# Modulation matmuls in column groups, a new load order, and scale and shift of a token tile in one VectorE pass

## The chip, the cores and the metric

The kernel runs on one core of a Trainium2 chip. The metric is the device time of one execution in microseconds; lower is better. The core has five engines with instruction rows of their own: PE (TensorE, matmuls and transposes), DVE (VectorE), ACT (ScalarE), POOL (GpSimd) and SP (SyncE, which here issues the DMAs). Each engine takes its instructions strictly in the order of its row, and one that waits for a semaphore holds up all behind it.

## The reference

One layer of a generator, batch 1, 1024 latent tokens (x) and 256 context tokens (ctx) of width 1024, all in fp32. The change touches only its beginning:

```python
mod_x = (silu_c @ w_ada[layer] + b_ada[layer])[:, None, :]
mod_c = silu_cc @ w_ada[layer] + b_ada[layer]
sh_m, sc_m, gt_m, sh_f, sc_f, gt_f = jnp.split(mod_x, 6, axis=-1)
csh_m, csc_m, cgt_m, csh_f, csc_f, cgt_f = jnp.split(mod_c, 6, axis=-1)
px = modulate(rms_norm(x, g_pre_mix[layer]), sh_m, sc_m) @ w_in[layer]
pc = modulate(rms_norm(ctx, g_pre_mix[layer]), csh_m, csc_m) @ w_in[layer]
```

`modulate(h, shift, scale)` is `h * (1 + scale) + shift`. Behind it come windowed attention, a bidirectional mLSTM, the output projection and a SwiGLU block, whose code is the same in both kernels.

## The kernel before, in words

**Precision.** A large product is made of three fast fp32r matmuls. Each operand is split into a high part (a cast on ScalarE) and a low part (raw minus high, a subtraction on VectorE); `mm3` (L74 to L79) adds high·high, high·low and low·high. In a trace the three carry the lines L77, L78 and L79.

**The modulation vectors** (L304 to L371). For section 1 (scale) and then section 0 (shift) of w_ada, eight row tiles `wa` of 128x1024 (512 KB) are loaded. silu(c) and silu(c_ctx) stand as columns in `cs4` (split) and `cz4` (plain fp32, two more columns zero). In each section three tiles (`PLAIN`, L304) are multiplied in plain fp32; the other five are split by ScalarE and VectorE (L65, L66), with the space of `hh` and `hl` as a scratch. The result `pr` (4 rows of 512, two tiles) is copied into `Vc` and transposed by PE to columns, `pcol`; VectorE adds the bias and leaves `scol` (scale) and `hcol` (shift), one value for each of the 1024 features.

**The token tiles.** There are ten tiles of 128 tokens, eight latent (0 to 7) and two context (8, 9). `prep_a` (L188) loads tile i, sums its squares on ScalarE, takes root and reciprocal, and for the tiles below XT = 6 multiplies by it on GpSimd (tile 2 on ScalarE). `prep_t` (L209) transposes it on PE: eight 128x128 transposes into two PSUM tiles `pt` of half a token tile each, of which there are two at a time (`tp`). `prep_m` (L227) multiplies by the scale on VectorE, one 128x512 pass per half; for tiles from 6 on a transposed copy is loaded and another form is used (L235). `prep_b` (L247) adds the shift (VectorE for tiles 0 and 1, GpSimd behind them), casts to `hh` on ScalarE and subtracts to `hl` on VectorE. `hh` and `hl` have two halves, of four feature blocks each.

**The slabs.** `s1(i)` (L404) multiplies token tile i by `w1` (272 columns: gates, attention V, the first mLSTM head's V): `slab`, eight blocks of three matmuls of 128x272. VectorE adds the gate biases (the two `G` passes), ScalarE copies `av` and `V` out. For slab 0 the order is another: all sixteen matmuls with hh (L391), then the eight with hl (L394). `s2(i)` (L419) multiplies by `w2` (384 columns, the other three heads' V) the first NFILL = 3 tiles; it is interleaved with s1 from i = 3. `w1` is split in `w1_split` (L291), in four casts and four subtractions of 128x544, `w2` at i = 1 and 2 (L452), in four casts and four subtractions of 128x768.

**What sets the order.** Engines' rows are laid down by a scheduler with estimates of its own; instructions in `tc.keep_in_program_order` stay in the order of the program on their engine; `tc.issue_after` holds a DMA back until the named instruction. SP issues the loads in this order: the scale section's eight tiles, two of the shift section, x0, x1, the other six, w1 (two loads), bcr, x2, x3, cst, x4, x5, and the w2 loads between the later tiles. Tiles 0 and 1 are transposed ahead of slab 0, among the shift section's matmuls.

Of the kernel before, what the change touches and what calls it, by code (L numbers as in the profile page):

```python
# [44 lines left out]
def body(tc, x, ctx, xtr, vecs, bcv, bada, gqm, gqf, wada, ws1, ws2, wt, wout, wfi, wfo,  # L45
# [132 lines left out]
    xts, hraw, xd = {}, {}, {}  # L178
# [6 lines left out]
    def prep_a2(i):  # L185
        tc.keep_in_program_order(act.activation(xts[i], xts[i], AF.Copy, scale=st[:, 10 + i:11 + i]))

    def prep_a(i, parts=(0, 1)):  # L188

        j = i - NT  # L190
        xt = xts[i] = R(4 + i % 4, f"xt{i}", (D,))
        xd[i] = dma(xt, x[i * P:(i + 1) * P] if i < NT else ctx[j * P:(j + 1) * P])
        hraw[i] = R((2, 3)[i] if i < 2 else (12, 13, 8, 9, 10, 11)[i % 6], f"hraw{i}", (KT, P))
        if i >= XT:
            dma(hraw[i], xtr[i - XT])
        sq = act.activation(xt if i >= XT else hraw[i].rearrange("p a b -> p (a b)"), xt, AF.Square, accum_out=st[:, i:i + 1])
        if i > 1:
            tc.keep_in_program_order(sq)
        if 1 not in parts:
            tc.keep_in_program_order(act.activation(st[:, 10 + i:11 + i], st[:, i:i + 1], AF.Sqrt, bias=epst, scale=1.0 / D))  # L200
            return
        rms_r(st[:, 10 + i:11 + i], st[:, i:i + 1])
        if i < XT:
            pool.tensor_scalar(xt, xt, st[:, 10 + i:11 + i], 1.0, MUL, MUL)
# [22 lines left out]
    def prep_m(i):  # L227

        if i not in pts:
            prep_t(i)  # L230
        rw = hraw.pop(i)
        raw2[i] = [rw[:, 4 * b:4 * b + 4] for b in range(2)]
        if i >= XT:
            for k in range(KT):
                dve.scalar_tensor_tensor(rw[:, k], rw[:, k], scol[:, i // NT, k:k + 1], pts[i], MUL, MUL)  # L235
            return
        for b in range(2):
            if i == 1 and not b:
                for k in range(4):
                    tc.keep_in_program_order(act.activation(raw2[i][b][:, k], pts[i][b][:, k], AF.Copy,  # L240
                                                                    scale=scol[:, 0, 4 * b + k:4 * b + k + 1]))
                continue
            r = dve.tensor_tensor(raw2[i][b], pts[i][b], hcast(scol[:, i // NT, 4 * b:4 * b + 4]), MUL)
            if i == 1:
                tc.keep_in_program_order(r)

    def prep_b(i):  # L247
# [7 lines left out]
        for b in (1, 0) if i == 0 else range(2):  # L255
            r = (dve if i < 2 else pool).tensor_tensor(raws_[b], raws_[b], hcast(hcol[:, q, 4 * b:4 * b + 4]), ADD)
            if i < 2:
                tc.keep_in_program_order(r)
            if i == 0:
                w1_split(1, (1 - b,))  # L260
        for b in range(2):
            h_ = hs[b][:, :, tok]
            if i + b == 0:
                for k in range(4):
                    act.activation(h_[:, k], pts[i][b][:, k], AF.Identity, scale=scol[:, q, k:k + 1],
                                   bias=hcol[:, q, k:k + 1])
            else:
                tc.keep_in_program_order(act.copy(h_, raws_[b]))
            r = dve.tensor_tensor(ls[b][:, :, tok], raws_[b], h_.bitcast(F32), SUB)
            if i == 0:  # L270
                tc.keep_in_program_order(r)
        if i == 0:
            with tc.issue_after(last):
                prep_a(2, (0,))
            r2 = st[:, 12:13]
            tc.keep_in_program_order(dve.reciprocal(r2, r2))
            prep_a2(2)
# [13 lines left out]
    def w1_split(i, part=None):  # L291

        if part is None or -1 in part:
            for k in (0, 2):
                r = act.copy(w1h[i][:, k:k + 2], w1r[i][:, k:k + 2])
                if part:
                    tc.keep_in_program_order(r)
        for k in (0, 1) if part is None else part if part[0] >= 0 else ():
            sl = slice(2 * k, 2 * k + 2)
            r = dve.tensor_tensor(w1l[i][:, sl], w1r[i][:, sl], w1h[i][:, sl].bitcast(F32), SUB)  # L300
            if part:
                tc.keep_in_program_order(r)

    PLAIN = {1: (0, 2, 4), 0: (0, 2, 7)}  # L304
    last, nsp, late = None, 0, []

    wm = pa.tile([P, 4, P], F32, name="warm", tag="mm", bufs=4)
    for i in range(11):
        pe.matmul(wm[:, i % 4], ones, ones, start=True, stop=True)
    for sec in (1, 0):  # L310
        pr = [pa.tile([4, 512], F32, name=f"pr{sec}{i}", tag="mm", bufs=4) for i in range(2)]
        for kt in range(KT):
# [10 lines left out]
            ops = [(kt, *o) for o in ops]  # L323
            if (sec, kt) > (0, 2) and not sec:
                late += ops
                ops = ()
            if (sec, kt) == (0, KT - 1):

                ops = late = [late[k] for k in (0, 2, 1, 4, 3, 6, 5, 8, 7)]
            for n, (k, a, b) in enumerate(ops):  # L330
                if late and n < 2:
                    prep_t(1, True, (n,))
                for i in range(2):
                    r = pe.matmul(pr[i], a[:, k, :], b[:, i * 512:(i + 1) * 512], start=kt == 0 and n == 0,
                                  stop=kt == KT - 1 and n == len(ops) - 1)
                    if late:
                        tc.keep_in_program_order(r)
            if (sec, kt) == (0, 1):
                for i in range(2):
                    with tc.issue_after(last):  # L340
                        prep_a(i)
                        last = xd[i].ins
            if (sec, kt) == (0, 2):
                prep_t(0, True)
            if (sec, kt) == (0, 7):
                prep_m(0)
                prep_m(1)
                for i in range(2):
                    with tc.issue_after(last):
                        last = w1_load(i)  # L350
                w1_split(0)
                with tc.issue_after(last):
                    last = dma(bcr, bcast(bcv)).ins
        r4 = Vc.rearrange("p n h v -> p (n h v)")[0:4, 0:D]
        r = act.copy(r4[:, 0:512], pr[0])
        if sec == 0:
            tc.keep_in_program_order(r)
            w1_split(1, (-1,))
        dve.tensor_copy(r4[:, 512:D], pr[1])
        pc_ = pa.tile([P, KT, 4], F32, name="pcol", tag="gx", bufs=2)  # L360
        for kt in range(KT):
            pe.transpose(pc_[:, kt, :], r4[:, kt * P:(kt + 1) * P], ident[0:4, 0:4])
        for q in range(2):
            t = (hcol, scol)[sec][:, q]
            if sec:
                dve.scalar_tensor_tensor(t, pc_[:, :, q], 1.0, bcol(1), ADD, ADD)
                dve.tensor_tensor(t, pc_[:, :, 2 + q], t, ADD)
                dve.tensor_tensor(t, t, vec[:, VGPM:VGPM + 8], MUL)
            else:
                for b in (bcol(0), t):  # L370
                    tc.keep_in_program_order(dve.tensor_tensor(t, pc_[:, :, q if b is not t else 2 + q], b, ADD))  # L371
# [32 lines left out]
    def s1(i):  # L404
        ps = slab(i, 272, w1h, w1l)
# [11 lines left out]
    w2h, w2l, s2ps = [], [], {}  # L417
# [11 lines left out]
    prep_b(0)  # L429
    prep_b(1)  # L430
    with tc.issue_after(xd[2].ins):
        prep_a(3, (0,))
    with tc.issue_after(xd[3].ins):
        dma(cst, const)
    for i in range(NI):
        if i + 4 < NI:
            prep_a(i + 4)
        if i == 0:
            s1(i)
            prep_t(2, True)  # L440
        if i + 2 < NI:
            prep_b(i + 2)
        if i == 0:
            r = st[:, 13:14]
            dve.reciprocal(r, r)
            tc.keep_in_program_order(pool.tensor_scalar(xts[3], xts[3], r, 1.0, MUL, MUL))
        if i:
# [1593 lines left out]
```

## Time and profile before

| what | value |
|---|---|
| median of 3 runs | 1171.96 us (1171.68 to 1172.77) |
| the profiled execution | 1171.69 us, span 1169.9 us from first to last instruction |
| mean granted TensorE clock | 0.998 of full speed |
| PE busy | 1155.5 us, 99% of the span |
| DVE, ACT, POOL busy | 782.8, 558.6, 154.5 us |
| slab 0 on PE | 33.94 to 39.27 us |
| slab 1 on PE | 40.14 to 43.23 us |
| HBM traffic over the span | 184 GB/s on average; some 410 GB/s from 5 to 39 us |

Times in the profile are microseconds from the span's start. A row of the timeline gives start, length, engine, line, operation, what it writes and reads, shape, and in brackets how long the engine stood idle before it and what ended that. Matmuls are pipelined: a record's length is a latency, and the distance between starts is the price.

### The profile page before, as it was taken

What the parts mean: (1) busy time and instruction counts of PE and PEld (TensorE: products, weight loads), DVE (VectorE), ACT (ScalarE), POOL (GpSimd) and SP (SyncE); (2) the same over time, 40 slices, a digit from 0 to 9 for tenths busy, and PEclk for the clock granted to TensorE, in tenths of its full rate; (3) what the DMA queues carried; (4) which work ended last, traced back from release to release, by engine and by line L of the source; (5) the groups of instructions that cost most, each with busy time, mean ns of one, the idle gap of its engine ahead of it and who ended that gap; (6) DMA issues with size and microseconds to landing.
All of it is one profiled execution on the core that took longest, in us unless ns stands there. A gap on an engine that the chain in (4) does not pass through costs nothing.

```text
span 1169.9 us, 16222 instructions
## 1 busy us (share of the span) xinstructions
PE 1155.5 (99%) x5857; PEld 945.5 (81%) x5857; DVE 782.8 (67%) x1391; ACT 558.6 (48%) x1037; POOL 154.5 (13%) x201
## 2 busy tenths in 40 slices
PE   9899999999999999999999999999999999999997
PEld 3799888878888767888788888888888888888886
DVE  5874768873787643479777777767677755644557
ACT  6753442223777855877543333334343344434533
POOL 1430001263664630000000000000000000000000
PEclk9999999999999999999999999999999999999999
DMA  9722954657797605220334556566645467665853
GB/s 367 281 68 80 391 175 144 210 170 230 206 254 202 174 10 198 90 83 26 99 135 171 199 206 241 212 201 219 222 143 161 150 212 273 201 208 191 307 181 126
DMA packets 103272, 216.99 MB, mean 185 GB/s; under 512 B 10260, under 2 KB 39572, under 8 KB 101784
## 3 DMA queue, kind: packets, MB, share of 16 engines
q1 hardware_dynamic: 103192, 215.95, 55.5%
q8 instruction: 46, 0.75, 0.3%
q14 instruction: 34, 0.28, 0.1%
HBM read 159.29 MB, written 55.97 MB: 184 GB/s over the span
## 4 chain that ended last, share of the span: by engine, by line
PE 95%; DMA 2%; DVE 2%; issue 0%; ACT 0%; SPq 0%; DVEq 0%
PE xv L79 8%; PE xv L77 8%; PE xv L78 8%; PE pt L78 6%; PE pt L79 6%; PE pt L77 6%; PE t L609 4%; PE t L611 4%; PE t L608 4%; PE pt L1063 3%; PE pt L1045 3%; PE op L77 3%; PE op L78 3%; PE op L79 2%; PE fx L77 2%; PE fx L79 2%
## 5 line engine op out<-in xcount | busy, mean ns | idle before, releaser
L66 DVE TENSOR_TENSOR fo<-fr,fo 128x1024 fp32r<-128x1024 f32 x77 | 92.8, 1223 | 71.4 <-ACT fo L65 69.9
L65 ACT CAST fo<-fr 128x1024 fp32r<-128x1024 f32 x77 | 79.5, 1049 | 74.1 <-PE pt L79 38.2
L608 PE MATMUL t<-hh,th 128*128 128x512 f32 x208 | 82.4, 396 | 0.0
L609 PE MATMUL t<-hl,th 128*128 128x512 f32 x208 | 82.0, 394 | 0.0
L1445 ACT CAST wS<-wr 128x512 fp32r<-128x512 f32 x88 | 54.2, 622 | 55.4 <-PE pt L79 36.8
L1447 DVE TENSOR_TENSOR wS<-wr,wS 128x512 fp32r<-128x512 f32 x88 | 60.4, 689 | 19.7 <-ACT wS L1445 19.7
L79 PE MATMUL xv<-tT,wS 128*128 128x512 f32 x168 | 65.6, 391 | 0.0
L77 PE MATMUL xv<-tT,wS 128*128 128x512 f32 x168 | 65.6, 391 | 0.0
L78 PE MATMUL xv<-tT,wS 128*128 128x512 f32 x168 | 65.5, 390 | 0.0
L611 PE MATMUL t<-hh,tl 128*128 128x512 f32 x208 | 65.0, 393 | 0.0
L77 PE MATMUL op<-woh,mh 128*128 128x512 f32 x128 | 50.9, 397 | 0.0
L79 PE MATMUL op<-woh,ml 128*128 128x512 f32 x128 | 50.0, 390 | 0.0
L78 PE MATMUL op<-wol,mh 128*128 128x512 f32 x128 | 50.0, 390 | 0.0
L1193 DVE TENSOR_TENSOR wr<-wr 128x512 f32<-128x512 f32 x66 | 45.5, 690 | 1.4
L608 PEld LDWEIGHTS t<-hh,th 128*128 128x128 f32 x208 | 39.1, 188 | 8.3 <-issue 0.3
L1479 ACT ACTIVATE es<-es 128x512 f32<-128x512 f32 x22 | 13.9, 633 | 66.6 <-DVE es L1196 66.5
L609 PEld LDWEIGHTS t<-hl,th 128*128 128x128 f32 x208 | 39.1, 188 | 8.0 <-issue 1.2
L77 PE MATMUL pt<-fo 128*128 128x512 f32 x110 | 42.8, 389 | 0.0
L78 PE MATMUL pt<-fo 128*128 128x512 f32 x110 | 42.8, 389 | 0.0
L79 PE MATMUL pt<-fo 128*128 128x512 f32 x110 | 42.8, 389 | 0.0
L611 PEld LDWEIGHTS t<-hh,tl 128*128 128x128 f32 x208 | 37.2, 188 | 6.5 <-issue 0.3
L782 PE MATMUL s<-k,qh 128*128 128x256 f32 (+1 forms) x128 | 41.6, 336 | 0.5 <-DVE sm L784 0.5
(788 smaller groups left out, 3339.3 us busy)
## 6 DMA issues: line engine op xcount, KB each, us to landing
wr<-in_wfi SPq DMA_DIRECT2D x44, 512.0 KB, 5.2
wb<-in_wada SPq DMA_DIRECT2D x24, 512.0 KB, 5.8
s_d<-a SPq DMA_DIRECT2D x22, 512.0 KB, 6.7
bt<-in_wfo SPq DMA_DIRECT2D x44, 256.0 KB, 3.4
tb_d<-bt SPq DMA_DIRECT2D x11, 1024.0 KB, 3.9
fr<-s_d SPq DMA_DIRECT2D x44, 256.0 KB, 4.4
fr<-tb_d SPq DMA_DIRECT2D x44, 256.0 KB, 4.6
fr<-a_d SPq DMA_DIRECT2D x33, 256.0 KB, 4.3
```

Source lines behind the costliest of these rows:

```text
L65: act.copy(hi, raw)
L66: dve.tensor_tensor(lo, raw, hi.bitcast(F32), SUB)
L77: pe.matmul(ps, a[0], b[0], start=first, stop=False, **kw)
L78: pe.matmul(ps, a[0], b[1], start=False, stop=False, **kw)
L79: pe.matmul(ps, a[1], b[0], start=False, stop=last, **kw)
L608: pe.matmul(o, wh[:, kt], m[0], start=f, stop=False)
L609: pe.matmul(o, wh[:, kt], m[1], start=False, stop=False)
L611: pe.matmul(o, wl[:, kt], m[0], start=False, stop=l)
L782: pe.matmul(o, qh[:, h, :], k2[g][:, kc], start=True, stop=False)
L1193: dve.tensor_tensor(out, a, b, SUB)
L1445: act.copy(w[:, 0], raw)
L1447: dve.tensor_tensor(w[:, 1], raw, w[:, 0].bitcast(F32), SUB)
```

## The change

**Modulation.** All sixteen w_ada tiles are multiplied in plain fp32, with `cz`, 32 columns of which two are used. A tile's two halves go to two groups of 32 PSUM rows and columns of the array, and odd row tiles to the other two groups: `pr[g:g+32]`, g = 32·(2·(kt mod 2) + i). One PSUM tile `pr` of 128x512 takes it all; it is copied in two 128x256 pieces and transposed in four 128x128 pieces, and VectorE adds even and odd groups. Small matmuls without use (`warm`, 32 rows, 128 columns) stand between the tiles and around the transposes. The ten casts and ten subtractions of w_ada tiles, the `PLAIN` table and `cs4` are gone.

**Loads.** Only x0 stands among the w_ada tiles. Behind them come w1, x1, x2, bcr, x3, x4, x5, cst, all four w2 pieces (each with a raw tile of its own), then the tiles from 6 on.

**Scale and shift.** For tiles 1 to 5, VectorE reads the transposed tile from PSUM and applies scale and shift in one `tensor_scalar` with two column operands, eight passes of 128x128 for a tile; the two 128x512 multiplications, and the GpSimd additions of tiles 2 to 5, are gone. Tile 0 has code of its own (`prep_b0`).

**Order.** Tile 1 is transposed behind slab 0; tile 2 inside slab 1, tile 4 inside slab 2 (`mid`), with tiles 3 and 5 behind these in the program. The w2 casts and subtractions move from i = 1, 2 to i = 2, 3. `ch`, `cl` are allocated at i = 4.

The core of the diff:

```diff
+    cz = q1.tile([P, KT, 32], F32, name="cz")
...
-            if kt in PLAIN[sec]:
-                ops = ((cz4, w),)
-            else:
-                wh, wl = (t[1 - nsp // 4 % 2][:, nsp % 4] for t in (hh, hl))
-                nsp += 1
-                split(wh, wl, w)
-                ops = ((cs4, wh), (cs4, wl))
...
+            for i in range(2):
+                g = 32 * (2 * (kt % 2) + i)
+                tc.keep_in_program_order(pe.matmul(pr[g:g + 32], cz[:, kt, :], w[:, i * 512:(i + 1) * 512],
+                                                   start=kt < 2, stop=kt > 5))
+            if kt < KT - 1:
+                warm(1)
             if (sec, kt) == (0, 1):
-                for i in range(2):
-                    with tc.issue_after(last):
-                        prep_a(i)
-                        last = xd[i].ins
+                with tc.issue_after(last):
+                    last = prep_l(0)
+                prep_c(0)
...
+            for f in (lambda: w1_load(0), lambda: w1_load(1), lambda: prep_l(1), lambda: prep_l(2),
+                      lambda: dma(bcr, bcast(bcv)).ins, lambda: prep_l(3)):
                 with tc.issue_after(last):
-                    last = dma(bcr, bcast(bcv)).ins
+                    last = f()
...
         for b in range(2):
+            if i:
+                for k in range(4):
+                    kk = 4 * b + k
+                    t = dve.tensor_scalar(rw[:, kk], pts[i][b][:, k], scol[:, 0, kk:kk + 1], hcol[:, 0, kk:kk + 1], MUL, ADD)
+                    tc.keep_in_program_order(t)
+                if i < 4 and b == (i > 1):
+                    prep_c((2, 4, 5)[i - 1], 1)
+            else:
+                dve.tensor_tensor(raw2[i][b], pts[i][b], hcast(scol[:, 0, 4 * b:4 * b + 4]), MUL)
...
     for i in range(NI):
...
         if i == 0:
+            s1(0)
+            prep_t(1, True)
+            prep_c(2, 0)
+            prep_b(1)
...
+        elif i < 3:
+            s1(i, lambda: prep_t(2 * i, True))
+            prep_b(2 * i)
...
+            prep_t(2 * i + 1, True)
+            prep_b(2 * i + 1)
...
-        if i in (1, 2):
-            b = i - 1
+        if i in (2, 3):
+            b = i - 2
```

VectorE's row of before around slab 1, from the end of slab 0 (tile 1 is `hraw_234`, tile 2 `hraw_350`; L243 is the multiplication by the scale, L269 hl, L408 and L410 the G passes):

```order
L408 TENSOR_TENSOR G<-slab,bcr 128x2x4
L410 TENSOR_TENSOR G<-slab,bcr 128x2x4
L269 TENSOR_TENSOR hl_103<-hraw_234,hh_101 128x4x128
L243 TENSOR_TENSOR hraw_350<-pt,scol 128x512
L269 TENSOR_TENSOR hl_104<-hraw_234,hh_102 128x4x128
L243 TENSOR_TENSOR hraw_350<-pt,scol 128x512
L445 RECIPROCAL st<-st 128x1
L408 TENSOR_TENSOR G<-slab,bcr 128x2x4
```

The same place now (tile 1 is `hraw_254`, tile 2 `hraw_257`; L250 is the new pass, L297 hl, L413 and L415 the G passes):

```order
L413 TENSOR_TENSOR G<-slab,bcr 128x2x4
L415 TENSOR_TENSOR G<-slab,bcr 128x2x4
L250 TENSOR_SCALAR hraw_254<-pt,scol,hcol 128x128 x4
L202 RECIPROCAL st<-st 128x1
L250 TENSOR_SCALAR hraw_254<-pt,scol,hcol 128x128 x4
L297 TENSOR_TENSOR hl_103<-hraw_254,hh_101 128x4x128
L297 TENSOR_TENSOR hl_104<-hraw_254,hh_102 128x4x128
L202 RECIPROCAL st<-st 128x1
L413 TENSOR_TENSOR G<-slab,bcr 128x2x4
L415 TENSOR_TENSOR G<-slab,bcr 128x2x4
L250 TENSOR_SCALAR hraw_257<-pt,scol,hcol 128x128 x8
```

In before tile 2 is multiplied between the hl passes of tile 1, ahead of slab 1's G; now the passes of tile 1 stand behind slab 0's G and those of tile 2 behind slab 1's.

ScalarE's row of before at the w2 casts (L460; L268 is a cast to hh, L196 a sum of squares, L412 and L413 the copies from a slab):

```order
L412 COPY av<-slab 128x128
L413 COPY V<-slab 128x128
L460 CAST w2h_477<-wr_0_479 128x768
L460 CAST w2h_477<-wr_2_483 128x768
L196 ACTIVATE xt_487,st<-xt_487 128x1024
L182 ACTIVATE st<-st,epst 128x1 x2
L268 CAST hh_101<-hraw_363 128x4x128
L412 COPY av<-slab 128x128
L413 COPY V<-slab 128x128
L268 CAST hh_102<-hraw_363 128x4x128
L460 CAST w2h_541<-wr_0_543 128x768
L268 CAST hh_101<-hraw_369 128x4x128
```

And now (L473 is the w2 cast, L296 the cast to hh, `hraw_361` is tile 4, `hraw_419` tile 5):

```order
L296 CAST hh_101<-hraw_361 128x4x128
L296 CAST hh_102<-hraw_361 128x4x128
L417 COPY av<-slab 128x128
L418 COPY V<-slab 128x128
L296 CAST hh_101<-hraw_419 128x4x128
L296 CAST hh_102<-hraw_419 128x4x128
L473 CAST w2h_528<-wr_00_421 128x768
L473 CAST w2h_528<-wr_02_423 128x768
L473 CAST w2h_563<-wr_10_425 128x768
L473 CAST w2h_563<-wr_12_427 128x768
```

The first w2 casts stood ahead of the casts of tile 3 (`hraw_363` of before); now all four stand together behind those of tile 5. On PE, the first matmul that reads w2h stands now behind the last transposes of tile 5 (`xt_417`), ahead of slab 4:

```order
L77 MATMUL slab<-w1h_118,hh_102 128x272
L78 MATMUL slab<-w1l_120,hh_102 128x272
L79 MATMUL slab<-w1h_118,hl_104 128x272
L229 MATMUL pt<-vec,xt_417 128x128 x4
L77 MATMUL slab<-w2h_528,hh_101 128x384
L77 MATMUL slab<-w1h_117,hh_101 128x272
L78 MATMUL slab<-w1l_119,hh_101 128x272
```

One matmul of s2 now stands at the head of slab 4; the next that reads w2h follows some twenty rows later.

More of the change, by code (lines that the diff above doesn't have):

```diff
@@ L194, in prep_a, with prep_c @@
         if i >= XT:
[L195 to L204, printed above, removed]
+            with tc.issue_after(w2d[min(i - XT, 1)]):
+                dma(hraw[i], xtr[i - XT])
+        return xd[i].ins
+    def prep_c(i, part=None):
+        xt, r = xts[i], st[:, 10 + i:11 + i]
+        if part in (None, 0):
+            pin = tc.keep_in_program_order if i else lambda r: r
+            pin(act.activation(xt if i >= XT else hraw[i].rearrange("p a b -> p (a b)"), xt, AF.Square,
+                               accum_out=st[:, i:i + 1]))
+            pin(act.activation(r, st[:, i:i + 1], AF.Sqrt, bias=epst, scale=1.0 / D))
+        if part in (None, 1):
+            rc = dve.reciprocal(r, r)
+            if part:
+                tc.keep_in_program_order(rc)
+            if i == 1:
+                tc.keep_in_program_order(act.activation(xt, xt, AF.Copy, scale=r))
+            elif i < XT:
+                pool.tensor_scalar(xt, xt, r, 1.0, MUL, MUL)
+    def prep_a(i):
+        prep_l(i)
+        prep_c(i)
     pts = {}
@@ L289, in w1_load, with w1_split, warm @@
         return dma(w1r[i], ws1[:, i]).ins
[L291 to L307, printed above, removed]
+    def w1_split(i):
+        for k in (0, 2):
+            tc.keep_in_program_order(act.copy(w1h[i][:, k:k + 2], w1r[i][:, k:k + 2]))
+        for k in (0, 2):
+            tc.keep_in_program_order(dve.tensor_tensor(w1l[i][:, k:k + 2], w1r[i][:, k:k + 2],
+                                                       w1h[i][:, k:k + 2].bitcast(F32), SUB))
+    last = None
+    pcols = {1: pa.tile([P, 4, P], F32, name="pcol", tag="gx", bufs=2)}
+    wm = pa.tile([P, 4, P], F32, name="warm", tag="gx", bufs=2)
     for i in range(11):
         pe.matmul(wm[:, i % 4], ones, ones, start=True, stop=True)
+    def warm(n):
+        for i in range(n):
+            tc.keep_in_program_order(pe.matmul(wm[0:32, i % 4], cz[:, 0, :], ones, start=True, stop=True))
     for sec in (1, 0):
-        pr = [pa.tile([4, 512], F32, name=f"pr{sec}{i}", tag="mm", bufs=4) for i in range(2)]
+        pr = pa.tile([P, 512], F32, name=f"pr{sec}", tag="mm", bufs=4)
         for kt in range(KT):
@@ L354, in body @@
-        r4 = Vc.rearrange("p n h v -> p (n h v)")[0:4, 0:D]
-        r = act.copy(r4[:, 0:512], pr[0])
-        if sec == 0:
[L357 to L362, printed above, removed]
+        rr = Vc.rearrange("p n h v -> p (n h v)")[:, 512 * sec:512 * sec + 512]
@@ L363, in body @@
+        for k in range(4):
+            tc.keep_in_program_order(pe.transpose(pcols[sec][:, k, :], rr[:, k * P:(k + 1) * P], ident))
+        if sec == 0:
+            warm(3)
+        pcv = pcols[sec].rearrange("p k (g c) -> p g k c", c=32)
         for q in range(2):
-            t = (hcol, scol)[sec][:, q]
+            if not sec and q:
+                prep_b0()
+            t = (hcol, scol)[sec][:, q].rearrange("p (i k) -> p i k", k=4)
+            b_ = bcol(sec).rearrange("p (i k) -> p i k", k=4)
@@ L402, in vrow, with s1 @@
         return V[:, i] if i < NT else Vc[:, i - NT]
-    def s1(i):
-        ps = slab(i, 272, w1h, w1l)
+    def s1(i, mid=None):
+        ps = slab(i, 272, w1h, w1l, mid)
         sf = i + 2 if i < NT else i - NT
@@ L416, in body @@
     NFILL = 3
-    w2h, w2l, s2ps = [], [], {}
+    w2h, w2l, s2ps, w2r = [], [], {}, {}
     def s2(i, bs=(0, 1)):
@@ L427, in s2 @@
             act.copy(vrow(i)[:, 1:4, 0:128], s2ps.pop(i)[:, 0:384].rearrange("p (h v) -> p h v", v=128))
[L429 to L434, printed above, removed]
+    wc = None
     for i in range(NI):
-        if i + 4 < NI:
-            prep_a(i + 4)
         if i == 0:
[L439 to L447, printed above, removed]
+            s1(0)
+            prep_t(1, True)
+            prep_c(2, 0)
+            prep_b(1)
+            prep_c(3)
+            with tc.issue_after(last):
+                prep_l(4)
+            prep_c(4, 0)
+        elif i < 3:
+            s1(i, lambda: prep_t(2 * i, True))
+            prep_b(2 * i)
+            if i == 1:
+                prep_l(5)
+                with tc.issue_after(xd[5].ins):
+                    last = dma(cst, const).ins
+                for b in range(2):
+                    for k in (0, 2):
+                        raw = w2r[b, k] = R((14 if not b else 0) + k // 2, f"wr384_{b}{k}", (2, 384))
+                        with tc.issue_after(last):
+                            last = w2d[b] = dma(raw, ws2[:, b, k:k + 2]).ins
+                prep_c(5, 0)
+            prep_t(2 * i + 1, True)
+            prep_b(2 * i + 1)
+        else:
+            if 3 < i < NI - 2:
+                prep_b(i + 2)
             s1(i)
```

121 lines of the change are left out of this document (51 added, 70 removed).

## The prediction

> **What bounds the kernel now.** I read the page first, then busy time by windows, then the chain that ended last through the opening, and single instructions for prices. On the page:
>
> ```profile
> span 1169.9 us, 16222 instructions
> PE 1155.5 (99%) x5857; PEld 945.5 (81%) x5857; DVE 782.8 (67%) x1391; ACT 558.6 (48%) x1037; POOL 154.5 (13%) x201
> ```
>
> PE (TensorE) idles only 14.4 us of the span. The change drops no matmul of the slabs, so it can win only PE idle time, PE work that something else could have done, and throttled clock. All three lie in the opening, by windows:
>
> ```profile
> 5.00:30.00 25.00, 23.24 (x90) 6.78 (x89) 16.37 (x22) 14.86 (x22) 2.24 (x2) 1.00 1.02 406
> 30.00:34.00 4.00, 2.22 (x13) 0.79 (x11) 2.89 (x9) 3.33 (x7) 0.11 (x1) 1.00 1.04 408
> ...
> 65.00:70.00 5.00, 5.00 (x37) 5.00 (x36) 5.00 (x19) 2.73 (x8) 3.29 (x5) 1.00 0.01 3
> ```
>
> The columns are busy PE, weight load, VectorE, ScalarE, GpSimd, then granted clock, DMA share and GB/s. From 5 to 34 us DMA is saturated at 406 to 408 GB/s, so 512 KB take 1.29 us; from 65 us PE has no gap that this change could close. The chain in order of time (start, length, what) passes through two loads and then PE:
>
> ```profile
> 9.34 8.96 DMA xt<-in_x
> 18.32 11.56 DMA wr<-in_ws
> ...
> 33.43 0.47 ACT hh L265
> 33.94 3.73 PE slab L391 x16
> 37.68 1.59 PE slab L394 x8
> 39.27 0.87 PE pt L220 x8
> 40.14 0.13 PE slab L77
> ...
> 43.09 0.14 PE slab L79
> 43.25 0.17 DVE G L408
> ```
>
> x0 and x1 stand among the w_ada tiles, w1_0 lands at 29.88, slab 0 runs from 33.94 to 39.27, slab 1 (24 matmuls, 0.129 each) from 40.14 to 43.23. What PE waits for from 33 to 70 us (engine, line, releaser: sum, times, longest):
>
> ```profile
> PE slab L79 <- DVE hl L269: 1.6, 2, 1.5
> ...
> PE slab L391 <- ACT hh L265: 1.0, 1, 1.0
> ...
> PE slab L77 <- ACT hh L268: 0.2, 1, 0.2
> ```
>
> The 1.0 lies ahead of slab 0. Behind it PE waits only 1.8 us: the tile stream is already nearly full.
>
> **The load phase.** The modulation matmuls of before, on PE's timeline, and the only column groups that this trace holds:
>
> ```profile
> 5.46 1.88 PE L334 MATMUL pr<-wa,cz 128*4 128x512 f32 x4
> ...
> 30.72 0.63 PE L334 MATMUL pr<-hl,cs 128*4 128x512 f32 x2
> ```
> ```profile
> 308.40 0.64 PE L1063 MATMUL pt<-ts__3048,av 128*64 128x512 f32 x1
> 308.40 0.64 PE L1063 MATMUL pt<-ts__2895,av 128*64 128x512 f32 x1
> 308.88 0.59 PE L1063 MATMUL pt<-ts__3048,av 128*64 128x512 f32 x1
> ```
>
> A tile in plain fp32 costs 1.88 us on PE today, as four records (each fp32 matmul is two passes). Two matmuls on different 64-column groups start in the same nanosecond, two passes each per 0.9 us. If groups of 32 columns do that too, a w_ada tile costs about 0.9, and a warm matmul, a quarter of the columns of one that costs 0.94, some 0.2: less than the 1.29 in which it arrives. The ten casts and ten subtractions then vanish from the load phase, and with them the backlog that let the last modulation matmul start only at 30.72. The load order takes x1's 512 KB from ahead of w1: w1_0 lands at 29.88 − 1.29 = 28.6, its neighbour w1_1 (544 KB) about 30.0, x1 about 31.3.
>
> ScalarE and VectorE prices for what follows:
>
> ```profile
> 29.90 1.19 ACT L295 CAST w1h<-wr 128x544 fp32r<-128x544 f32 x2 [1.76 <-DMA wr<-in_ws]
> 33.43 1.50 ACT L265 ACTIVATE hh<-pt,hcol,scol 128x128 fp32r<-128x128 f32 x4 [0.61 <-DVE hcol L371]
> 34.81 0.63 ACT L268 CAST hh<-hraw 128x512 fp32r<-128x512 f32 x1
> 35.32 1.08 ACT L196 ACTIVATE hraw<-xt 128x1024 f32<-128x1024 f32 x1
> 36.28 0.21 ACT L196 ACTIVATION_READ_ACCUMULATOR hraw<-xt 128x1 f32 x1
> 36.52 0.29 ACT L200 ACTIVATE st<-st,epst 128x1 f32<-128x1 f32 x1
> 37.46 1.15 ACT L186 ACTIVATE xt<-xt,st 128x1024 f32<-128x1024 f32 x1 [0.64 <-DVE st L276]
> ...
> 52.54 0.83 ACT L460 CAST w2h<-wr 128x768 fp32r<-128x768 f32 x1 [0.94 <-DMA wr<-in_ws]
> ```
> ```profile
> 36.06 1.29 DVE L269 TENSOR_TENSOR hl<-hraw,hh 128x512 fp32r<-128x512 f32 x2
> 37.26 0.16 DVE L276 RECIPROCAL st<-st 128x1 f32<-128x1 f32 x1
> ...
> 61.36 1.62 DVE L235 SCALAR_TENSOR_TENSOR hraw<-hraw,scol,pt 128x128 f32<-128x128 f32 x6
> ...
> 65.14 0.21 DVE L451 TENSOR_SCALAR mF<-cst 128x128 f32<-128x128 f32 x1
> 65.27 0.22 DVE L451 TENSOR_SCALAR mB<-cst 128x128 f32<-128x128 f32 x1
> ```
>
> Slab 0: w1_0 28.6, its two casts to 29.8, first hh quarter 0.47, so PE starts at 30.3. ScalarE is done with hh0 at 31.3, with w1_1's casts at 32.5, with hh1 at 33.1. VectorE then has four passes of 0.65 and a reciprocal (half of w1l1, a shift addition, hl of both halves), ready at 35.3; four matmuls later slab 0 ends at **35.9, 3.4 us ahead of 39.27**.
>
> **The tile stream.** The new pass is an instruction that the kernel already has on another stage, from PSUM with two column operands:
>
> ```profile
> 541.15 1.36 DVE L1274 TENSOR_SCALAR mix<-pt,sfc,hfc 128x128 f32<-128x128 f32 x4
> 542.43 0.68 DVE L1196 TENSOR_TENSOR es<-es,po 128x512 f32<-128x512 f32 x1
> ```
>
> Four take 542.43 − 541.15 = 1.28, 0.32 each, 2.56 for the eight of a tile (TS below). A tile on VectorE is then 2.56 + 1.29 (hl) + 0.25 (two G at the pitch of such small ones) + 0.16 = 4.26 us; on PE it is 3.1 + 0.87 = 3.97. So VectorE, which used to leave half of the modulation to GpSimd, becomes the slower of the two. GpSimd's additions no longer matter to anyone.
>
> [...]
>
> Now tile by tile, in the order that the program sets (rows in the section on the change). I take handoffs as nothing.
>
> - Tile 1 isn't transposed before slab 0 any more. Its square follows hh1 on ScalarE: 33.1 + 1.2 + 0.29, reciprocal, + 1.15 = 35.9; transposes 35.9 to 36.8 (half by 36.4). First four TS to 37.7, cast 0.63: slab 1 starts at 38.4, **wait 1.6**. After two matmuls it needs hl: TS to 39.0, + 0.65 = 39.65, **wait 1.0**. With x2's transposes inside, slab 1 ends at 43.35, where before it ended at 43.23. The head start is gone.
> - Tile 2: VectorE has G of slab 1 ahead of TS, and G waits for slab 1's end; behind it wait all of TS and PE. G to 43.6, four TS to 44.95: x3's transposes need the PSUM buffer, **wait 1.6**. Then cast **0.2**, second half **0.4**, hl **0.35**. Slab 2 ends at 49.9.
> - Tiles 3 and 4: VectorE, never idle now, gives hl(3) at 51.1 and 53.6: **waits 0.05 and 0.5**. Slab 3 ends at 54.9, x5's last transposes at 55.35.
> - The next matmul in PE's row reads w2h. Its cast stands on ScalarE behind both casts of tile 5, these behind TS(5), this behind hl(4) and G of slab 3. From 53.6: three TS, hl, G, hl to 56.1; eight TS to 58.7; cast 59.35; w2h 0.83 to 60.2. **Wait 4.85**, with all of slab 4 queued behind. Before, those casts stand among the tile casts and are early.
>
> Sum: −3.4 for slab 0's end, +0.87 for x1's transposes, which now lie behind it, +10.55 of waits, −1.8 that before waits: **+6.2 us**. The loads behind tile 1 (x2 to x5, cst, w2: some 4 MB, 10 us at that rate) end well before 55 us and cost nothing.
>
> Bounds: VectorE is in an unbroken row from 43.4 to 58.7 with 32 TS, and 8 more matter in tile 1. At the 0.27 of L235 the sum loses up to 2.0; at 0.36 it grows by 1.6. Below 0.29 a tile costs VectorE less than PE, so further savings are lost in part.
>
> **The rivals.**
>
> *The clock drops as well.* In the windows of before:
>
> ```profile
> 35.00:36.00 1.00, 1.00 (x6) 0.79 (x5) 1.00 (x2) 1.00 (x2) 0.00 (x0) 0.72 1.04 414
> 36.00:37.00 1.00, 1.00 (x6) 1.00 (x5) 1.00 (x3) 0.79 (x3) 0.00 (x0) 0.50 1.01 406
> ...
> 38.00:39.00 1.00, 1.00 (x7) 1.00 (x7) 0.61 (x2) 1.00 (x2) 0.00 (x0) 0.57 1.03 399
> ```
>
> After PE's thin stretch at 31 to 34 the clock is halved for some 3.4 us, which costs about 1.7. The new wait of 4.85 is longer and emptier. One drop there gives 7.9, 1179.6 + 0.3; another in slab 1 gives up to 1.7 more. [...]
>
> *Nothing to measure.* If TS costs what L451 shows from SBUF (65.27 − 65.14 = 0.13), PE bounds the stream; tile 1 still waits some 1.0, G and TS of tile 2 another 1.0, w2h 0.25 + 0.65 + 1.04 + 0.63 + 0.83 − 0.44 = 3.0. That makes −3.4 + 0.87 + 5.0 − 1.8 = +0.7, 1172.7. Against it: L451 reads no PSUM and no column.
>
> *Faster.* PE bounds the stream and its waits stay at the 1.8 of before: −3.4 + 0.87 = −2.5, 1169.4. This decides if TS stays below 0.29 and ScalarE reaches w2h before PE does; the order speaks against the second at any price of TS.
>
> *The groups don't run side by side*, so the change doesn't do what it says. Then a tile costs 1.88 + 0.2, above 1.29: 16 of them from 5.46, with x0's transposes and the columns, end near 41 and not 27, and slab 0 starts some 13 later. Tile 1 is then ready (−4): about 1187. Against it: L1063.
>
> **How the numbers follow.** The sum is made on the profiled run, 1171.7, which is 0.3 under the median: 1171.7 + 6.2 + 0.3 = 1178.2. Chances: the sum without a further drop 0.38, with drops 0.34, nothing to measure 0.14, faster 0.07, groups in turn 0.05, the rest (later order) 0.02. A measurement can tell about 0.2%, 2.3 us. Slower: 0.38 + 0.34 + 0.05, with the slow end of the neutral case, 0.78; same 0.14; faster 0.08. The range goes from 1172.5, the neutral case's near end, to 1182.0, two drops.
>
> **What would show it.** Right: slab 0 ending near 36, slab 1 within 1 us of 43.2, TS at 0.32, one PE wait of 4 to 5 us released by a w2h cast, nothing changed behind 90 us. Wrong: a stream without PE gaps, TS near 0.13, w2h cast ahead of its matmul, or modulation matmuls in turn.

## The result and the profile after

Four runs of each kernel: the changed kernel takes 1189.24 us (1186.59 to 1189.77), the kernel before 1172.37 us (1171.68 to 1174.69). The ratio is 1.0136, interval [1.0115, 1.0157]: slower, as forecast, but by 16.9 us and not by 6, and outside the range. The profiled executions that are compared below took 1189.63 and 1171.69 us, a difference of 17.94 us.

The changed kernel's page, span and engines:

```profile
span 1187.8 us, 16250 instructions
PE 1159.6 (98%) x5887; PEld 951.9 (80%) x5887; DVE 769.8 (65%) x1409; ACT 549.9 (46%) x1024; POOL 141.3 (12%) x193
```

PE's idle time grew from 14.4 to 28.2 us, and its busy time by 4.1 us. The first is waits; the second is, for the most part, matmuls that run at half clock, as the windows of the changed kernel show (columns as in the prediction):

```profile
30.00:34.00 4.00, 2.74 (x18) 2.13 (x16) 3.77 (x7) 3.86 (x8) 0.00 (x0) 1.00 0.79 303
34.00:40.00 6.00, 3.43 (x23) 2.58 (x21) 4.79 (x18) 4.02 (x10) 1.12 (x1) 0.99 0.21 72
40.00:45.00 5.00, 4.33 (x19) 4.33 (x20) 1.47 (x4) 3.30 (x7) 1.12 (x1) 0.50 0.97 341
45.00:50.00 5.00, 3.30 (x19) 2.82 (x17) 2.63 (x10) 1.05 (x3) 0.00 (x0) 0.83 0.88 357
50.00:55.00 5.00, 4.89 (x28) 4.79 (x28) 4.97 (x14) 2.66 (x6) 1.42 (x1) 0.66 0.42 132
...
60.00:65.00 5.00, 0.66 (x2) 0.67 (x3) 4.87 (x12) 2.96 (x7) 0.00 (x0) 0.88 0.54 184
65.00:70.00 5.00, 5.00 (x31) 5.00 (x30) 3.04 (x5) 3.88 (x7) 0.00 (x0) 0.78 0.33 105
...
270.00:280.00 10.00, 8.10 (x41) 6.19 (x40) 6.47 (x13) 3.73 (x5) 8.42 (x15) 0.83 0.74 226
```

Read the number behind the five pairs, the granted clock: the rows with 0.50, 0.66 and 0.78 stand behind rows in which PE worked 3.43 of 6.00, 3.30 of 5.00 and 0.66 of 5.00 us. The trace's record of the clock has it halved from 39.9 us for 6.8 us, from 50.1, from 63.8 and from 275.4 for 3.4 us each; before had one such stretch, at 35.4 (and both kernels have one that begins in the last 1.3 us). From 60 to 65 us PE works 0.66 us.

The waits of PE from 28 to 120 us, changed kernel:

```profile
PE slab L77 <- ACT w2h L473: 4.4, 1, 4.4
PE slab L77 <- ACT hh L296: 1.8, 1, 1.8
PE pt L229 <- DVE hraw L250: 1.7, 1, 1.7
PE slab L394 <- ACT hh L277: 1.1, 1, 1.1
PE slab L79 <- DVE hl L297: 1.0, 1, 1.0
```

Every large one is a wait that the prediction had, at its place; the 1.1 lies inside slab 0, where the prediction had it as the time at which the second half of hh is ready. Their starts on PE's timeline, with slab 0's first matmul, its last eight and x1's transposes:

```profile
30.65 0.39 PE L394 MATMUL slab<-w1h,hh 128*128 128x272 f32 x1 [0.18 <-ACT hh L273]
...
34.96 1.42 PE L397 MATMUL slab<-w1h,hl 128*128 128x272 f32 x8 [0.40 <-DVE hl L268]
36.22 1.09 PE L229 MATMUL pt<-vec,xt 128*128 128x128 f32 x8
39.12 0.39 PE L77 MATMUL slab<-w1h,hh 128*128 128x272 f32 x1 [1.81 <-ACT hh L296]
...
40.67 0.59 PE L79 MATMUL slab<-w1h,hl 128*128 128x272 f32 x1 [1.03 <-DVE hl L297]
...
41.29 0.43 PE L78 MATMUL slab<-w1l,hh 128*128 128x272 f32 x1
...
47.05 0.29 PE L79 MATMUL slab<-w1h,hl 128*128 128x272 f32 x1
49.03 0.63 PE L229 MATMUL pt<-vec,xt 128*128 128x128 f32 x4 [1.70 <-DVE hraw L250]
```

Slab 0 ends at 36.2, 3.1 us ahead of before; slab 1 ends at 47.2, 4 us behind before, with two waits ahead of and in it and with matmuls that start 0.23 us apart from 39.9 to 46.7 and 0.13 apart behind that (records of 0.43 and 0.29).

**Where the 17.9 us came from.** I follow the lag of the changed kernel at two marks in PE's row: the first `t<-hh,th`, with which the projections behind the slabs begin, and the first `s<-k,qh`, with which the scores begin. Before, then after:

```profile
118.26 0.39 PE L608 MATMUL t<-hh,th 128*128 128x512 f32 x1
...
283.70 0.38 PE L782 MATMUL s<-k,qh 128*128 128x256 f32 x1
```
```profile
129.78 0.39 PE L626 MATMUL t<-hh,th 128*128 128x512 f32 x1
...
300.94 0.38 PE L800 MATMUL s<-k,qh 128*128 128x256 f32 x1
```

The lag is 11.5 us at the first mark, 17.2 at the second, 17.9 at the end. So the opening costs nearly twice what I summed, and some 6 us are lost between 120 and 300 us, where I had expected nothing. The opening splits into waits and work in two windows, from slab 0's end to the first mark, before and after:

```profile
39.27:118.26 78.99, 77.12 (x515) 74.37 (x514) 52.50 (x153) 40.25 (x87) 25.89 (x25) 1.00 0.36 115
```
```profile
36.22:129.78 93.56, 84.33 (x525) 81.16 (x524) 53.03 (x174) 41.12 (x88) 16.78 (x18) 0.93 0.33 107
```

PE idles 9.2 us here and 1.9 in before, 7.4 more; the sum had 10.55 − 1.8. It is busy for 7.2 us more, of which x1's transposes are 1.1. The other 6.1 are close to the 6.8 that 13.6 us at half clock can lose at most: this is the term that the sum does not have. What PE waits for behind the opening, from 120 to 330 us, in the changed kernel:

```profile
PE pu L735 <- DVE mkc L731: 2.8, 2, 1.9
PE s L965 <- DVE sm L802: 1.1, 1, 1.1
PE pk L729 <- ACT mkc L648: 0.9, 1, 0.9
```

### The profile page after: what moved, and what is told of

It reads as the page before. It is cut to its first block, busy times and chain, and to the rows that moved or that the text cites. A ratio compares the mean times of both kernels' runs of the same rounds, so it can differ in the third digit from the quotient of the medians.

```text
span 1187.8 us, 16250 instructions
## 1 busy us (share of the span) xinstructions
PE 1159.6 (98%) x5887; PEld 951.9 (80%) x5887; DVE 769.8 (65%) x1409; ACT 549.9 (46%) x1024; POOL 141.3 (12%) x193
## 4 chain that ended last, share of the span: by engine, by line
PE 87%; DVE 5%; DMA 3%; issue 2%; ACT 1%; POOL 1%; SPq 1%; DVEq 0%; ACTq 0%; POOLq 0%
PE xv L77 8%; PE xv L79 8%; PE xv L78 8%; PE pt L77 6%; PE pt L78 6%; PE pt L79 6%; PE pt L1081 3%; PE pt L1063 3%; PE op L77 2%; PE op L78 2%; PE op L79 2%; PE t L629 2%; PE t L627 2%; PE t L626 2%; PE slab L77 2%; PE slab L79 2%
```

## The experiments

All intervals are of the ratio to the kernel before, in runs on the same chip. "Lag" is the time by which a mark comes later than in before, in one profiled execution of each: at the first `t<-hh,th` (the opening), at the first `s<-k,qh`, and at the end of the span. The median of a kernel's runs lies up to 2.2 us from its profiled execution (e2_w2_early: 1184.43 and 1182.25).

| run | ratio to before | lag: opening | scores | end |
|---|---|---|---|---|
| the change | 1.0136 [1.0115, 1.0157] | 11.5 | 17.2 | 17.9 |
| e1_groups | 1.0011 [1.0003, 1.0020] | 1.2 | 1.4 | 2.1 |
| e2_w2_early | 1.0101 [1.0087, 1.0116] | 6.1 | 9.9 | 10.6 |
| e3_fill | 1.0101 [1.0082, 1.0119] | 7.2 | 10.1 | 11.0 |
| e4_old_tiles | 1.0154 [1.0138, 1.0170] | 14.6 | 18.3 | 19.0 |
| e5_later_pins | 1.0105 [1.0091, 1.0119] | 11.6 | 11.2 | 11.9 |
| e6_g_order | 1.0121 [1.0107, 1.0135] | 10.5 | 14.0 | 14.7 |
| e7_x1_early | 1.0150 [1.0136, 1.0163] | 14.1 | 18.0 | 18.7 |
| e8_all | 1.0059 [1.0045, 1.0073] | 6.9 | 7.1 | 7.8 |
| e9_groups_hcol | 1.0014 [1.0005, 1.0023] | 0.0 | 0.3 | 1.2 |
| e10_mended | 1.0049 [1.0034, 1.0063] | 4.8 | 4.2 | 5.9 |
| e11_fused_only | 1.0022 [1.0012, 1.0032] | 2.9 | 2.9 | 2.9 |
| e12_groups_fill | 1.0012 [1.0004, 1.0021] | 0.8 | 0.8 | 2.4 |

**How much of the opening is the clock: e3_fill.** Small matmuls without use are put into the changed kernel where PE waits; no wait is taken away.

```diff
             prep_t(1, True)
+            warm(7)
...
+            if i == 1:
+                warm(7)
             prep_t(2 * i + 1, True)
+            if i == 2:
+                warm(18)
```

> The changed kernel, with idle PE filled by small matmuls without use: 7 behind tile 1's transposes, 7 ahead of tile 3's, 18 behind tile 5's. Same waits, but PE is not thin. If the halved clock windows come from the waits and cost what their length says, the clock stays at 1.00 in the opening and the time falls by 5 us, to about 1184. Rival, a slower PE only fills time that it would have waited: falls by 1 us or less, 1188.

The two worst windows of this kernel, clock 1.00 where the changed kernel had 0.50 and 0.88:

```profile
40.00:45.00 5.00, 4.15 (x33) 4.00 (x34) 1.87 (x7) 3.30 (x7) 1.28 (x2) 1.00 0.98 376
60.00:65.00 5.00, 4.61 (x38) 4.34 (x37) 4.87 (x8) 4.61 (x7) 0.00 (x0) 1.00 0.32 91
```

The opening's lag falls from 11.5 to 7.2. So the halved stretches cost 4.3 us there, and what is left, 7.2, is the sum of the prediction (6.2) plus 1. It is less than the 6.1 us of slower work above; part of that work took the place of waits, it seems, which no run shows apart.

**The longest wait alone: e2_w2_early.** The first two w2 casts go ahead of tile 5's casts.

```diff
+            if i == 2:
+                w2_split(0)
             prep_t(2 * i + 1, True)
...
-        if i in (2, 3):
...
+        if i == 3:
+            w2_split(1)
```

> The changed kernel, with the first two w2 casts ahead of tile 5 instead of behind it. If the 4.4 us wait of PE is only ScalarE's order, it shrinks below 1.5 us, the halved clock behind it goes, and the time falls by 4 to 6 us, to about 1184. Rival, VectorE is the bound of the stream, so the wait moves to the low part of tile 4 or 5: falls by under 2 us.

The first matmul with w2h waits for 0.4 us, where the changed kernel waited 4.43:

```profile
59.05 0.44 PE L77 MATMUL slab<-w2h,hh 128*128 128x384 f32 x1 [0.37 <-ACT w2h L442]
```

The opening's lag falls by 5.4 us, more than the 4.0 by which the wait shrank: two stretches of 3.4 us at half clock are left in it (from 41.7 and from 48.5), none behind the w2h wait, where the changed kernel had four. Not all of that is the edit's doing: one that went lay in slab 1, and e5_later_pins, whose opening is the changed kernel's, has three. The place of one cast in ScalarE's row made the dearest single wait of the opening.

**Is the dear thing the new pass? e4_old_tiles, e6_g_order, e11_fused_only.** First the changed kernel with the old form of scale and shift:

```diff
             if i:
-                for k in range(4):
...
+                tc.keep_in_program_order(dve.tensor_tensor(raw2[i][b], pts[i][b], hcast(scol[:, 0, 4 * b:4 * b + 4]), MUL))
...
-        if i >= XT:
-            for b in range(2):
-                h_add(raws_[b], q, b, pool)
+        for b in range(2):
+            r = h_add(raws_[b], q, b, dve if i < 2 else pool)
```

> The changed kernel, with scale and shift of tiles 1 to 5 as before: two 128x512 multiplications on VectorE, the additions on VectorE for tile 1 and on GpSimd for 2 to 5. If the price of the eight small passes makes the stream VectorE-bound, the waits of tiles 2 to 5 and for w2h fall, and the time by 5 us or more. Rival, the order (tile 1 behind slab 0, G ahead of a tile's pass, w2 behind tile 5) makes them whatever the pass costs: falls by 2 us at most, and a wait of some 4 us for w2h stays.

PE's two longest waits in this kernel:

```profile
PE slab L77 <- ACT w2h L471: 5.0, 1, 5.0
PE slab L77 <- ACT hh L294: 4.4, 2, 3.9
```

It is no faster, as the rival had it: the wait for w2h stays, so the order alone is enough for that one. It is no clean price of the pass, though. The wait of 3.9 is for tile 1's `hh`, whose additions VectorE makes here, behind a reciprocal for which it waits 1.0 itself; the other one, 0.45, is for a cast that waits for GpSimd's additions. Next, the changed kernel with the pass of tiles 2 and 4 ahead of `G`:

```diff
-            s1(i, lambda: prep_t(2 * i, True))
+            s1(i, lambda: (prep_t(2 * i, True), prep_m(2 * i)))
```

> The changed kernel, with scale and shift of tile 2 (and 4) placed ahead of the G passes of the slab in which they are transposed. If tile 2's wait of 1.7 us comes from VectorE waiting for slab 1's end, it goes below 0.5, and a halved clock window with it: 3 us faster at the first projection. Rival, VectorE is simply too slow for the tile stream: the wait moves to the next tile and under 1 us is gained.

Tile 2's wait falls from 1.7 to 0.5 us, but the opening by only 1.0 and not by 3: it still has 13.6 us at half clock, and PE waits 0.5 at the transposes of tile 5 and 4.7 for w2h. Last, before with the new pass alone, for tiles 2 to 5:

```diff
+            if i > 1:
+                for k in range(4):
+                    kk = 4 * b + k
+                    dve.tensor_scalar(rw[:, kk], pts[i][b][:, k], scol[:, 0, kk:kk + 1], hcol[:, 0, kk:kk + 1], MUL, ADD)
+                continue
...
-        for b in (1, 0) if i == 0 else range(2):
+        for b in (1, 0) if i == 0 else () if 1 < i < XT else range(2):
```

> The kernel before with the fused VectorE pass for tiles 2 to 5 alone (8 passes of 128x128 in place of two of 128x512 and GpSimd's additions); order, loads and modulation of before. If the pass at 0.32 us makes VectorE the slower engine of the stream (4.26 us a tile against 3.97 on PE), 1 to 3 us slower. Rival, GpSimd's additions slowed VectorE as much: within 0.5 us of before, or faster.

It is 2.9 us slower: the pass has a price of its own in before's order. PE waits for it, and the clock is halved once more, at 51.7. Its longest wait:

```profile
PE pt L220 <- DVE hraw L246: 2.6, 2, 2.0
```

The pass takes the time that I gave it. VectorE in the changed kernel:

```profile
47.37 0.17 DVE L413 TENSOR_TENSOR G<-slab,bcr 128x8 f32<-128x8 f32 x1 [5.13 <-PE slab L79]
...
47.52 2.63 DVE L250 TENSOR_SCALAR hraw<-pt,scol,hcol 128x128 f32<-128x128 f32 x8
50.08 0.15 DVE L202 RECIPROCAL st<-st 128x1 f32<-128x1 f32 x1
```

From 47.52 to 50.08 eight passes make 2.56 us, 0.32 each. Ahead of them VectorE stands idle for 5.13 us, until slab 1 ends: the passes stand behind `G`, which needs that slab.

**What the column groups alone bring: e1_groups, e9_groups_hcol, e12_groups_fill.** Before with the modulation in column groups and hh of tile 0 ahead of w1_1's casts; tiles 0 and 1 are transposed somewhat later among the shift tiles, and loads, tile stream and w2 stay:

```diff
-    PLAIN = {1: (0, 2, 4), 0: (0, 2, 7)}
...
-        pr = [pa.tile([4, 512], F32, name=f"pr{sec}{i}", tag="mm", bufs=4) for i in range(2)]
+        pr = pa.tile([P, 512], F32, name=f"pr{sec}", tag="mm", bufs=4)
```

> The kernel before, with one part of the change alone: modulation in column groups (and its warm matmuls), and hh of tile 0 made ahead of the casts of the second half of w1; loads, tile stream and w2 as in before. If the loss comes from the new tile stream and not from the groups, slab 0 starts at 31.5 (33.9 before), ends at 36.7 (39.3), and the kernel is 2 us faster than before, about 1170. Rival, any head start is given back by the stream: within 0.5 us of before. Second rival, the groups or their warm matmuls cost something of their own: slower than before.

No gain. On VectorE w1l's two passes had come ahead of `hcol`, so slab 0 started at 33.72 (before: 33.94). The next run puts `hcol` first:

```diff
         if i == 0:
+            w1_split(0, (-1,))
+            w1_split(0, (0, 1))
...
-            w1_split(0)
```

> As e1 (the kernel before with column groups), with hcol made on VectorE ahead of the low part of w1, which in e1 stood ahead of it. If only that row kept slab 0 of e1 at 33.7 us, it starts at 32.7 and ends at 38.3, 1 us before the kernel before, and the time is 1 to 2 us below e1, at or under before. Rival, the tile stream gives it back again: same as e1 or before within 0.5 us.

Slab 0 starts at 32.59, 1.35 earlier than in before, and ends at 39.0, 0.3 earlier: the half clock came at 35.7. The third run adds filler matmuls.

```diff
+                warm(10)
...
-            warm(3)
+            warm(5)
...
+                if kt == 4:
+                    warm(4)
```

> As e9 (column groups in the kernel before, hcol first), with PE kept busy by matmuls without use: 10 where x0 and x1 are awaited, 2 more behind the columns, 4 between the halves of slab 0. In e9 slab 0 started 1.35 us earlier than before and then ran at half clock until 39.1. If that window is what ate the head start, slab 0 ends near 37.5 and the kernel is 1 to 2 us faster than before, 1170. Rival, the tile stream waits for that much more behind it: same as before.

The windows from 35 to 39 us of the second kernel, then of the third:

```profile
35.00:39.00 4.00, 3.77 (x17) 3.66 (x18) 3.58 (x7) 3.10 (x7) 0.00 (x0) 0.59 1.02 403
```
```profile
35.00:39.00 4.00, 3.48 (x23) 2.58 (x21) 3.94 (x10) 3.10 (x6) 0.00 (x0) 1.00 1.03 407
```

With the clock held, slab 0 ends near 38.3, 1 us earlier than in before, and the stream behind gives it back: PE then waits 1.3 us for `hl` (1.5 in before) and 1.4 for `w2h` (nothing in before). All three kernels are slower than before by a little over 0.1%.

**x1 back ahead of slab 0: e7_x1_early.** In the changed kernel, x1 is loaded behind x0, transposed among the shift tiles, and its passes stand right behind tile 0's.

```diff
-                with tc.issue_after(last):
-                    last = prep_l(0)
-                prep_c(0)
+                for i_ in range(2):
+                    with tc.issue_after(last):
+                        last = prep_l(i_)
+                    prep_c(i_, 0)
+                    prep_c(i_, 1)
...
+            if (sec, kt) == (0, 6):
+                prep_t(1, True)
```

> The changed kernel, with x1 loaded behind x0 again, transposed before slab 0, and scaled and shifted right behind tile 0 on VectorE. Slab 0 starts 1.3 us later (512 KB). If tile 1 behind slab 0 makes the waits of 1.8 and 1.0 us and the first long halved window (6.8 us), these go and the time falls by 3 us. Rival, the later start costs as much as the waits: no gain.

Missed: the opening's lag grew to 14.1. ScalarE's row in this kernel shows why:

```profile
40.50 0.27 ACT L421 COPY av<-slab 128x128 f32<-128x128 f32 x1 [3.81 <-DVE hcol L381]
...
40.82 1.15 ACT L296 CAST hh<-hraw 128x512 fp32r<-128x512 f32 x2
```

The cast of tile 1's hh stands behind the `av` copy of slab 0. That copy follows `G` of slab 0 (the bracket names the small pass right behind it), which stands on VectorE behind tile 1's eight passes and runs at 40.18; slab 0 ended at 39.05, and the first half of tile 1 was ready for its cast at 38.85. ScalarE is idle for 3.81 us, slab 1 waits 2.5, and the clock is halved for 10.2.

**The later loss: e5_later_pins.** In the changed kernel the exponentials of the mLSTM weights are kept ahead of the first silu on ScalarE, and the later w_ada loads behind the last of the weight loads on SP. Nothing in the opening is touched.

```diff
-            dma(w, bcast(a_d[r0:r0 + 4, :].rearrange("(o h) t -> o (h t)", o=1)).rearrange("p (h t) -> p h t", h=4))
+            wld.append(dma(w, bcast(a_d[r0:r0 + 4, :].rearrange("(o h) t -> o (h t)", o=1)).rearrange("p (h t) -> p h t", h=4)))
...
-            act.activation(w, w, AF.Exp)
+            tc.keep_in_program_order(act.activation(w, w, AF.Exp))
...
-            act.activation(d, t, AF.Silu)
+            tc.keep_in_program_order(act.activation(d, t, AF.Silu))
...
-        with tc.issue_after(twd[j].ins):
+        with tc.issue_after(twd[j].ins), tc.issue_after(wld[-1].ins):
```

> The changed kernel; the opening untouched. Behind it the exponentials of the mLSTM weights are pinned ahead of the first silu on ScalarE, and the loads of later w_ada tiles wait for the last weight load. The lag behind the kernel before was 11.5 us at the first transposed projection and 17.2 us where the attention scores begin. If the loss in between comes from the row in which the scheduler put these weights (last exponential at 165.6 us, two more table loads), it falls by 3 us or more and the time to 1185. Rival, it is a consequence of the late opening itself (data late, not order): under 1 us.

The lag now stays: 11.6 at the end of the opening, 11.2 at the scores, 11.9 at the end; the span is 1181.8, 6.0 us shorter than the changed kernel's (the medians differ by 4.6). The halved stretch and PE's waits between the marks are gone. ScalarE's row shows what had changed. In before, the last exponential (L550) is at 140.06 and then come the silu's table load and the silu (L630):

```profile
140.06 0.63 ACT L550 ACTIVATE w<-w 128x512 f32<-128x512 f32 x1 [0.37 <-DVE w L549]
140.72 1.28 ACT L630 ACT_TABLE_LOAD   x1
...
150.80 0.42 ACT L630 ACTIVATE mkc<-ct 128x256 f32<-128x256 f32 x1 [4.00 <-DVE ct L629]
```

In the changed kernel the first silu (L648) stands between the exponentials (L568), and the table is loaded three times:

```profile
152.82 1.28 ACT L648 ACT_TABLE_LOAD   x1
155.48 1.06 ACT L648 ACTIVATE mk<-ct 128x1024 f32<-128x1024 f32 x1 [1.37 <-DVE ct L647]
...
158.35 1.28 ACT L568 ACT_TABLE_LOAD   x1
...
165.59 0.63 ACT L568 ACTIVATE w<-w 128x512 f32<-128x512 f32 x1 [0.42 <-DVE w L567]
...
174.89 1.28 ACT L648 ACT_TABLE_LOAD   x1 [2.65 <-DMA w_dr<-w]
176.18 0.42 ACT L648 ACTIVATE mkc<-ct 128x256 f32<-128x256 f32 x1
```

`mkc`, a key tile, comes 25.4 us later than in before, where the kernel as a whole was 11.5 behind; its second half, at 183.17, is 24.5 late. On SP the last loads `w<-a_d` of these weights go out behind eight of the `wb` loads (two in before). PE waits 0.9 us for that second half, at 183.64, and 0.95 at 184.91 for what VectorE makes of it (L731, under the same name). A later wait for L731, of 1.90 us, is followed by 3.4 us at half clock from 275.4:

```profile
272.40 0.39 PE L627 MATMUL t<-hl,th 128*128 128x512 f32 x1
274.68 1.35 PE L735 MATMUL pu<-V,mkc 128*64 128x129 f32 x16 [1.90 <-DVE mkc L731]
...
276.98 0.63 PE L626 MATMUL t<-hh,th 128*128 128x512 f32 x1
```

These three waits (3.7 us) and the halved stretch (1.7 at most) make 5.4 of the 5.7 us by which the lag grew between the two marks. How the last of them hangs together with the late key tile was not followed; e3, e4, e6 and e7, with the same row, don't have it. The 0.7 behind the scores is another matter: e5 keeps it. In the other kernels with this row (e2, e3, e4, e6, e7) it grew from the opening to the end by 3.8 to 4.7 (e2 and e3 without a halved stretch behind the opening, the others with one near 190 us). Which of the two, exponentials or loads, does more was not tried apart.

**Together: e8_all and e10_mended.** The first takes e2, e5, e6 and e7; the second, whose edit of the opening follows, e2, e5 and two of the fillers of e3.

```diff
+            warm(7)
...
+            if i == 2:
+                w2_split(0)
+            else:
+                warm(7)
             prep_t(2 * i + 1, True)
```

> The four together: x1 early, tile 2 ahead of G, w2 casts ahead of tile 5, later order pinned; column groups and the fused pass stay. If order makes the loss and the parts add (3 + 3 + 5 + 3, less what they share), the time is 1173 to 1177. If the fused pass is a VectorE bound of its own, it stays above 1180.

> The changed kernel with w2 casts ahead of tile 5, filler matmuls behind tile 1 and ahead of tile 3, and the pinned later order. If the losses are the wait for w2h, the halved clock and the later row, and add up: 17.9 - 5 - 3 - 5.5 is about 4 us over before, 1176. Rival, there is a loss of the fused pass that none of these touch: over 1180.

Both came out slower than expected. The first, 1179.25 us, keeps e7's fault (3.1 us of wait for tile 1's hh, and half clock for 6.8). The second, 1177.85 us, has no halved stretch and no loss between the marks, and its opening still lags by 4.8 us. Of these 1.5 are there when slab 1 ends (44.74, in before 43.22); the rest was not followed, but e11 shows that the pass alone, with one more halved stretch, cost before 2.9. No version of the changed kernel beats before.

What stays open: behind the scores every kernel with the column groups loses 0.7 us or more, e12 and e10 1.6 and 1.7. Some 11 us behind that mark PE waits 1.1 us for `sm` in all of them (L965 above), and 0.3 in before and e11, which have no column groups. Why, was not followed.

## Why the prediction was right and wrong

**Right, by its steps.** Slab 0: start 30.3 and end 35.9 forecast, 30.65 and 36.2 measured. The groups run side by side: a tile at about 0.9 us forecast, 0.88 from the row at 10.63 to the next. The pass at 0.32 us, from the same form in a later stage, 0.32 measured. The waits: 1.6, 1.0, 1.6 and 4.85 forecast at four places, 1.81, 1.03, 1.70 and 4.43 measured, each with the releaser named. Only the small ones, 1.5 together, are hardly there; why is not shown (slower slabs might leave VectorE time, but e3_fill, at full clock, lacks them too). With the clock held (e3_fill) the opening costs 7.2 us; the sum said 6.2. That VectorE is the slower one of the stream was not tested by itself: a run that takes the eight passes out (e4_old_tiles) changed tile 1's way as well.

**Wrong, first: the clock.** The likeliest case had no more halved stretches than before, and the rival at most two. The opening had 13.6 us at half clock, four stretches of 3.4 against one in before. The step that failed is "the clock drops as well" as a rival beside the sum: the sum itself made four waits of 1 us and more close together, and with PE kept busy in those waits (e3_fill) the clock stayed at 1.00. It should have been a term, +4.3 us by e3_fill. I had also counted on the wait of 4.85 as the likely place, and it gave one stretch; slab 1, behind the thin 34 to 40 us with its waits, had two. How many there are is partly luck: three of the four runs had a mean clock of 0.991 or 0.992 and took 1188.86 us or more, the fourth 0.995 and 1186.59.

**Wrong, second: "nothing changed behind 90 us".** "The rest (later order)" had a chance of 0.02. It cost 6 us between the profiled executions, 4.6 between the medians (e5_later_pins). The rows of ScalarE and SP had changed there, and that could be read without a chip: the order of both kernels showed the exponentials on the other side of the silu. I had compared the rows of the opening only. The scheduler lays down the whole program, and moving loads at its start moved SP's row far behind it.

**The account.** From the forecast 1178.2 to 1189.24: +1.0 in the sum, +4.3 for the clock, +6.4 behind the opening (5.7 up to the scores, which e5 mends, and 0.7 behind them, which it doesn't), −0.7 since the median stands 0.4 under the profiled run and not 0.3 over it. With the later order mended (e5_later_pins, 1184.68) or the clock held (e3_fill, 1183.43) the time still lies above the range's 1182.0: either error alone carries it out.

## What to carry to other kernels

When a scheduler lays down the rows, compare the whole order, not the stretch that was edited: a table load or a DMA that changed sides far behind the edit is part of the change (here two table loads more on ScalarE, 1.28 us each, and a key tile 25.4 us later). Four PE waits of 1 us and more near each other came here with 13.6 us at half clock, which cost 4.3 us: such a term belongs in the sum. And a head start is worth only what the next serial chain leaves of it: here slab 0 ended 3 us earlier and slab 1 stood for tile 1, whose transposes, passes and casts lay behind slab 0; the dearest single wait came from a cast that stood in its engine's row behind work that was needed later.

## What the runs showed of the hardware

- The half clock came in pieces of 3.41 us on one grid: the trace's record of the clock gives 3.413 for each of the stretches from 50.1, 63.8 and 275.4 and 6.827 for the one from 39.9, and the later three starts lie 3, 7 and 69 pieces after the first. The piece ahead of 275.4 was not idle as a whole: in it PE idled for 1.90 us (272.8 to 274.7) and was busy for the rest. Laid over this grid, the fourteen profiles of this case agree with one another: from full clock, each piece in which PE idled for 1.9 us or more was followed by a halved one (in the changed kernel 2.07 ahead of 39.9, 3.41 ahead of 63.8, 1.90 ahead of 275.4), none with 1.1 or less was, and between these both came (1.45 in before was not, 1.15 in e9_groups_hcol was). There is one exception, the stretch that begins at 193.4 in e6_g_order: the piece ahead of it has no idle time, but sixteen matmuls of a single column take 1.95 us of it. So idle time alone doesn't settle it.
- With filler matmuls of 32 columns the clock was 1.00 through the whole opening in the profiled executions of e3_fill, e10_mended and e12_groups_fill; their mean granted clock is 0.999, the changed kernel's 0.992.
- Plain fp32 matmuls in different groups of 32 columns ran side by side. In before the four records of a plain tile took 1.88 us, and the next row started 1.81 later (9.54 to 11.35); here is one of the changed kernel, with the next row on PE 0.88 later.

```profile
10.63 1.05 PE L339 MATMUL pr<-wa,cz 128*32 128x512 f32 x4 [0.22 <-DMA wa<-in_wada]
11.51 0.38 PE L329 MATMUL warm<-ones,cz 128*32 128x128 f32 x2
```
